# RMSNorm and matmul on one core: sixteen words of the output written at the outset, x in half-group loads throughout, finer last stores

## The chip, the cores and the metric

The kernel runs on one core of a Trainium2 chip. Its time is the device time of one execution in microseconds (us). Its compute engines are TensorE (PE), VectorE (DVE), ScalarE (ACT) and GpSimd (POOL); SyncE (SP) only waits and issues transfers. All transfers between the chip's main memory (HBM) and the on-chip buffer (SBUF) are carried by the core's 16 DMA engines.

## The reference

```python
batch, seq, dim, out_dim = 16, 1024, 512, 768

def reference(x, gamma, weight, eps):
    rms = np.sqrt(np.mean(x ** 2, axis=-1, keepdims=True) + eps)
    x_norm = x / rms * gamma
    return np.matmul(x_norm, weight).astype(np.float32)
```

x is 16384 rows (tokens) of 512 float32, 33.6 MB; the weight is 512 by 768 float32, 1.6 MB; the output is 16384 rows of 768 float32, 50.3 MB.

## The kernel before

**Tiling.** The rows form 128 tiles of 128 rows, and two tiles are a pair (`j`, tiles `2j` and `2j+1`). x is loaded in groups of 16 tiles (`XG`), the output is stored in groups of 8 (`OG`). Row numbering inside a group is `(p t)`: in x group 3, for instance, partition p holds 16 consecutive rows, one for each of the group's tiles. There are two x buffers (`xt`, 16 tiles each) and three output buffers (`ot`, 8 tiles each). `stretches` (L126) says in which pieces a group is transferred: x group 0 in loads of 2, 2, 4 and 8 tiles; groups 1, 2, 5, 6 and 7 in two loads of 8; groups 3 and 4, which the table leaves out, in one load of 16. Output group 0 goes in stores of 2, 2 and 4 tiles, group 1 and the last one (15) in two stores of 4, all others in one store of 8.

**Work on a tile.** POOL casts x to bf16. Three quarters of the tiles are turned by PE (transposes against the identity, L228) and copied out of PSUM by DVE (L237); the last four tiles of each group from the second on are turned by DVE alone (L269). ACT squares and sums each row (L194) and takes roots (L199), DVE takes the reciprocal (L201). PE multiplies by the weight, into which gamma has been folded at the start: four weight loads and eight matmuls a tile (L294, L298). `finish_tile` scales a result by the row's reciprocal root into `ot`: even tiles on ACT (L277), odd ones on DVE (L279). The last tile of each store also waits for the tile before it, so that one wait covers the store.

**Queues and order.** The order of work is written out by hand and recorded in `Order`: each operation names the cells that it reads and writes, and `emit` (L39) places a wait where an engine does not yet know that a needed operation has ended. `known` holds, for each engine, what it knows to be done: of engines a count, of transfers their own key. Transfers take a semaphore from a pool of slots. `last` (L81) collects the transfers that nobody awaits; `emit` returns their marks, and SP waits for those at the very end (L437). All loads and stores are issued by SP in program order, but for gamma's, which ACT issues first of all (L338), before it loads its activation table (L339). `load_until` issues the loads of x groups while tiles are worked on; `store(i)` (L286) issues a store when the last tile of its stretch is done. What SP waits for holds up everything behind it on SP.

Of the kernel before, what the change touches and what calls it, by code (L numbers as in the profile page):

```python
# [11 lines left out]
F32 = mybir.dt.float32  # L12
# [4 lines left out]
P = 128  # L17
# [3 lines left out]
class Order:  # L21
# [17 lines left out]
    def emit(self):  # L39
        nc = self.tc.nc  # L40
        streams = {id(e): n for n, e in enumerate((nc.tensor, nc.vector, nc.scalar, nc.gpsimd, nc.sync))}
        writer, readers = {}, {}
        known = [dict() for _ in streams]
        clocks, needs, place, slot_of, slots = [], [], [], {}, []
        count = [0] * len(streams)
        for n, (proc, engine, _, reads, writes) in enumerate(self.ops):
            at = streams[id(engine)]
            if proc is None:
                me, turn = ("transfer", n), 1
            else:  # L50
                count[at] += 1
                me, turn = at, count[at]
            written = {writer[cell] for cell in reads + writes if cell in writer}
            read = {d for cell in writes for d in readers.get(cell, ())}
            need = []
            for d in sorted(written | read, reverse=True):
                who, when = place[d]
                if who == me and (engine is nc.tensor or d not in written):
                    continue
                if known[at].get(who, 0) < when:  # L60
                    need.append(d)
                    for k, v in clocks[d].items():
                        known[at][k] = max(known[at].get(k, 0), v)
            if proc is None:
                free = [k for k, d in enumerate(slots) if known[at].get(("transfer", d), 0)]
                if free:
                    slots[free[0]] = n
                else:
                    slots.append(n)
                slot_of[n] = ("slot", slots.index(n))  # L70
            clock = dict(known[at])
            clock[me] = turn
            place.append((me, turn))
            clocks.append(clock)
            needs.append(need)
            for cell in reads:
                readers.setdefault(cell, []).append(n)
            for cell in writes:
                writer[cell], readers[cell] = n, []
        awaited = {d for need in needs for d in need}  # L80
        last = [n for n, (me, _) in enumerate(place) if not isinstance(me, int) and n not in awaited]  # L81
        sems, marks, done = {}, {}, {}
        for n in range(len(self.ops)):
            me = slot_of.get(n, place[n][0])
            if n in slot_of or n in awaited:
                if me not in sems:
                    sems[me] = self.tc.alloc_semaphore(f"done{len(sems)}")
                done[me] = done.get(me, 0) + (16 if n in slot_of else 1)
                marks[n] = (sems[me], done[me])
        for n, (proc, engine, issue, _, _) in enumerate(self.ops):  # L90
            for d in needs[n]:
                engine.wait_ge(*marks[d])
            ins = issue()
            if n in marks:
                ins.then_inc(marks[n][0], 16 if n in slot_of else 1)
        return [marks[n] for n in last]
# [3 lines left out]
def kernel(  # L100
# [8 lines left out]
    nc = tc.nc  # L109
    PE, DVE, ACT, POOL, SP = nc.tensor, nc.vector, nc.scalar, nc.gpsimd, nc.sync  # L110
    order = Order(tc)

    def run(engine, issue, reads=(), writes=()):
        order.add(1, engine, issue, reads, writes)

    x = x.flatten_outer_dims()
    out = out.flatten_outer_dims()
    N, D = x.shape
    _, O = out.shape
    K = D // P  # L120
    NT = N // P
    NP = NT // 2
    XG, OG = 16, 8
    AHEAD = 20

    def stretches(group, parts):  # L126
        first, size, i = {}, {}, 0
        for g in range(NT // group):
            for n in parts.get(g, [group]):
                for t in range(i, i + n):  # L130
                    first[t], size[t] = i, n
                i += n
        return first, size

    last = NT // OG - 1
    x_first, x_size = stretches(XG, {0: [2, 2, 4, 8], **{g: [8, 8] for g in (1, 2, 5, 6, 7)}})
    o_first, o_size = stretches(OG, {0: [2, 2, 4], 1: [4, 4], last: [4, 4]})

    def rows(ap, i, n):
        base, t = (x_first[i], x_size[i]) if i < XG else (i - i % XG, XG)  # L140
        return ap[base * P:(base + t) * P, :].rearrange("(p t) d -> p t d", t=t)[:, i - base:i - base + n, :]

    def sb(name, shape, dtype):
        return nc.alloc_sbuf_tensor(name, shape, dtype).ap()
# [14 lines left out]
    ot = [sb(f"ot{n}", [P, OG, O], F32) for n in range(3)]  # L159
# [7 lines left out]
    def cells(name, slot, i, n=1):  # L167
        return [(name, slot, t) for t in range(i, i + n)]
# [117 lines left out]
    def store(i):  # L286
        first, n = o_first[i], o_size[i]
        s = first // OG % 3
        if i == first + n - 1:
            src = ot[s][:, first % OG:first % OG + n, :]  # L290
            order.transfer(SP, lambda: SP.dma_start(out=rows(out, first, n), in_=src), reads=cells("ot", s, first % OG, n))

    def hold(lhsT, cell):
        run(PE, lambda: PE.ldweights(lhsT), [cell])  # L294
# [20 lines left out]
    def finish_tile(i, a, engine):  # L315
        s = i // OG % 3

        before = [("ot", s, i % OG - 1)] if i == o_first[i] + o_size[i] - 1 else []
        scale(engine, ot[s][:, i % OG, :], ops[a][:, :O], rstd[:, i:i + 1],
              [("ops", a, 0), ("ops", a, 1), ("rstd", i)] + before, [("ot", s, i % OG)])  # L320
        store(i)
# [14 lines left out]


    order.transfer(ACT, lambda: ACT.dma_start(out=g_row, in_=gamma.rearrange("(h w c) -> h w c", w=P, c=2)), writes=["g_row"])  # L338
    run(ACT, lambda: ACT.preload_act_table(AF.Sqrt))  # L339
    wv = weight.rearrange("(h w c) o -> w h (c o)", w=P, c=2)  # L340

# [131 lines left out]
```

## Time and profile before

| | us |
|---|---|
| median of 4 runs | 209.61 (209.52 to 210.35) |
| the profiled execution's own time | 209.52 |
| its span, first to last instruction | 207.6 |
| last compute instruction ends (DVE, L279) | 199.36 |
| last store issued by SP | 199.38 |
| last store landed (6.8 after its issue) | 206.2 |

| engine | busy us | share of the span |
|---|---|---|
| PE (matmul) | 194.5 | 94% |
| DVE | 149.4 | 72% |
| ACT | 144.6 | 70% |
| POOL | 59.9 | 29% |
| DMA, SP's queue | | 97.4% of 16 engines |

The mean granted TensorE clock is 0.984. The transfers move 85.62 MB at a mean of 412 GB/s. Busy time says how much of the span an engine worked, not that it set the end: where two resources are both nearly always busy, one must look at which of them works last, and at whether it ever stood idle before. A transfer has three moments: its issue on SP, its first packets on the DMA engines, and its landing, when its completion is counted on a semaphore.

### The profile page before, as it was taken

The numbers are of one execution on the slowest core, as the hardware profiler recorded it, in microseconds if no ns is written. First come the engines' busy times: TensorE is split into PE (matmuls) and PEld (weight loads), VectorE is DVE, ScalarE is ACT, GpSimd is POOL, SyncE is SP. The second block draws the span as 40 slices with busy tenths as digits, with TensorE's granted clock in tenths as the row PEclk, the third lists the DMA queues.
The fourth block names the chain that finished last, engine by engine and source line by source line (L and its number), as shares of the span: only waits on it lengthen the run. The fifth ranks groups of instructions, "written<-read, shape, count | busy, mean of one in ns | idle before, by whom it ended". The sixth has DMA issues, their size and how long they took to land.

```text
span 207.6 us, 2784 instructions
## 1 busy us (share of the span) xinstructions
PE 194.5 (94%) x1236; PEld 72.6 (35%) x717; DVE 149.4 (72%) x255; ACT 144.6 (70%) x343; POOL 59.9 (29%) x34
## 2 busy tenths in 40 slices
PE   7789999999999999999999999999999999999920
PEld 1223434433343333343334333443343334433300
DVE  0446466999579975999569975999569974999410
ACT  3598898777787687776877687677877788663310
POOL 2055742046200291005800670006600273000000
PEclk9999999999999999999999999999999999999985
DMA  6999999999999899999999999999999999997995
GB/s 221 398 445 436 369 410 436 428 429 422 438 458 442 368 439 429 448 395 447 425 420 429 428 440 425 412 437 429 439 409 433 425 453 410 445 421 298 450 381 230
DMA packets 5488, 85.62 MB, mean 412 GB/s; under 512 B 610, under 2 KB 612, under 8 KB 1380
## 3 DMA queue, kind: packets, MB, share of 16 engines
q1 hardware_dynamic: 5472, 85.46, 97.4%
q8 instruction: 7, 0.11, 0.2%
q14 instruction: 5, 0.04, 0.0%
q10 hardware_dynamic: 4, 0.00, 0.0%
HBM read 35.13 MB, written 50.33 MB: 412 GB/s over the span
## 4 chain that ended last, share of the span: by engine, by line
PE 89%; DMA 4%; SPq 1%; POOL 1%; DVE 0%; issue 0%
PE ps L298 78%; PE ps L228 10%; DMA xt<-in_x_dram 4%; SPq L343 1%; POOL xb L186 1%; DVE ot L279 0%; SPq L175 0%; SPq L468 0%; SPq L432 0%
## 5 line engine op out<-in xcount | busy, mean ns | idle before, releaser
L298 PE MATMUL ps<-w_bf,xT 128*128 128x512 bf16 (+1 forms) x800 | 147.6, 326 | 1.5 <-DVE w_bf L279 1.4
L277 ACT ACTIVATE ot<-ps,rstd 128x768 f32<-128x768 f32 x64 | 57.5, 899 | 43.6 <-PE ps L298 41.9
L194 ACT ACTIVATE jk<-xt 128x512 bf16<-128x512 f32 x128 | 78.8, 619 | 5.5 <-DMA xt<-in_x_dram 5.5
L186 POOL CAST xb<-xt 128x2048 bf16<-128x2048 f32 (+3 forms) x21 | 46.3, 2218 | 112.3 <-DMA xt<-in_x_dram 77.0
L279 DVE TENSOR_SCALAR ot<-ps,rstd 128x768 f32<-128x768 f32 x64 | 64.8, 1013 | 8.5 <-PE ps L298 7.8
L294 PEld LDWEIGHTS <-xT 128*128 128x128 bf16 x400 | 39.3, 98 | 60.0 <-issue 52.1
L228 PE MATMUL ps<-ident_f,xb 128*128 128x128 f32 x200 | 54.5, 277 | 0.9 <-POOL xb L186 0.9
L237 DVE COPY xT<-ps 128x1024 bf16<-128x1024 bf16 (+1 forms) x53 | 34.5, 654 | 25.1 <-PE ps L228 23.4
L269 DVE STREAM_TRANSPOSE xTq<-xq 32x256 f32<-32x256 f32 x112 | 48.8, 435 | 3.4
L228 PEld LDWEIGHTS ps<-ident_f,xb 128*128 128x128 f32 x200 | 28.2, 143 | 46.7 <-issue 43.2
L298 PE MATMUL ps<-w_bf,xTq 128*128 128x512 bf16 x224 | 42.8, 326 | 0.0
L194 ACT ACTIVATION_READ_ACCUMULATOR jk<-xt 128x1 f32 x128 | 24.3, 190 | 0.0
L294 PEld LDWEIGHTS <-xTq 128*128 128x128 bf16 x112 | 11.0, 98 | 14.5 <-issue 14.5
L258 POOL CAST xq<-xt 128x2048 bf16<-128x2048 f32 x7 | 13.3, 1893 | 0.0
L201 DVE RECIPROCAL rstd<-rms 128x8 f32<-128x8 f32 (+3 forms) x20 | 3.9, 192 | 7.4 <-ACT rms L199 7.2
L199 ACT ACTIVATE rms<-ssq,eps_sb 128x8 f32<-128x8 f32 (+3 forms) x20 | 6.0, 300 | 0.6
L298 PE MATMUL ps<-warm 128*128 128x512 bf16 x10 | 4.5, 590 | 1.4 <-DVE eps_sb L352 1.4
L277 ACT ACTIVATE w_bf<-w_f,g_sb 128x768 bf16<-128x768 f32 x2 | 1.9, 936 | 2.0 <-DMA w_f<-in_weight_dram 2.0
L375 DVE COPY g_sb<-ps 128x4 f32<-128x4 f32 x1 | 0.2, 163 | 3.1 <-PE ps L369 3.1
L279 DVE TENSOR_SCALAR w_bf<-w_f,g_sb 128x512 bf16<-128x512 f32 (+2 forms) x3 | 1.4, 482 | 1.5 <-DMA w_f<-in_weight_dram 1.5
L339 ACT ACT_TABLE_LOAD x1 | 1.3, 1283 | 1.5 <-SPq L432 1.5
L369 PEld LDWEIGHTS ps<-ident_f,g_row 2*128 2x128 f32 x2 | 0.3, 200 | 2.6 <-issue 2.6
(10 smaller groups left out, 2.0 us busy)
## 6 DMA issues: line engine op xcount, KB each, us to landing
out_dram<-ot SPq DMA_DIRECT2D x13, 3072.0 KB, 15.5
xt<-in_x_dram SPq DMA_DIRECT2D x11, 2048.0 KB, 20.0
xt<-in_x_dram SPq DMA_DIRECT2D x2, 4096.0 KB, 22.1
out_dram<-ot SPq DMA_DIRECT2D x5, 1536.0 KB, 10.1
w_f<-in_weight_dram SPq DMA_DIRECT2D x2, 768.0 KB, 6.1
out_dram<-ot SPq DMA_DIRECT2D x2, 768.0 KB, 14.8
xt<-in_x_dram SPq DMA_DIRECT2D x2, 512.0 KB, 5.4
xt<-in_x_dram SPq DMA_DIRECT2D x1, 1024.0 KB, 9.3
```

Source lines behind the costliest of these rows:

```text
L186: run(POOL, lambda: POOL.tensor_copy(out=xb[s][:, i % 8:i % 8 + n, :], in_=src), of, cells("xb", s, i % 8, n))
L194: run(ACT, lambda: ACT.activation(out=jk[j], in_=src[:, 0, :], func=AF.Square, accum_out=ssq[:, i:i + 1]), of, [("jk", j), ("ssq", i)])
L199: run(ACT, lambda: ACT.activation(out=rms[:, s], in_=ssq[:, s], func=AF.Sqrt, scale=1.0 / D, bias=eps_sb), [("ssq", t) for t in range(i, i ...
L201: run(DVE, lambda: DVE.reciprocal(out=rstd[:, s], in_=rms[:, s]), [("rms", i)], [("rstd", t) for t in range(i, i + n)])
L228: run(PE, lambda: PE.transpose(out=tp[b][:, t, h, :], in_=words[:, lo:lo + P], identity=ident_f), cells("xb", s, j % 4 * 2 + t) + ["ident" ...
L237: run(DVE, lambda: DVE.tensor_copy(out=dst[:, t:t + n, :], in_=src[:, t:t + n, :]), [("tp", b)], cells("xT", j % 4, t, n))
L258: run(POOL, lambda: POOL.tensor_copy(out=xq[s], in_=src), of, [("xq", s)])
L269: run(DVE, lambda: DVE.transpose(out=dst, in_=src), [("xq", s)], [("xTq", s)])
L277: run(ACT, lambda: ACT.mul(out=dst, in_=src, mul=r), reads, writes)
L279: run(DVE, lambda: DVE.tensor_single_scalar(out=dst, in_=src, scalar=r, op=mybir.AluOpType.mult), reads, writes)
L294: run(PE, lambda: PE.ldweights(lhsT), [cell])
L298: run(PE, lambda: PE.add_instruction(mybir.InstMatmult(name=nc.get_next_instruction_name(), engine=mybir.EngineType.PE, ins=[PE.lower_ap(r ...
```

## The change

The output's rows 0, 8, ..., 120 get a zero in their first column right after gamma's load, from ACT's queue; the first store (tiles 0 and 1, rows 0 to 255), which writes the same places, names the cell `marks` as written too, so that it waits for the sixteen words. x groups 3 and 4 are loaded in two halves like the others. Output group 14 goes in two stores of 4 tiles, group 15 in 4, 2 and 2. In `emit`, `last` is computed from the transfers that no engine's clock holds, instead of from those that nobody needs.

```diff
@@ emit
         awaited = {d for need in needs for d in need}
-        last = [n for n, (me, _) in enumerate(place) if not isinstance(me, int) and n not in awaited]
+        seen = {who for clock in known for who in clock}
+        last = [n for n, (me, _) in enumerate(place) if me not in seen and not isinstance(me, int)]
@@ tile_rmsnorm_matmul_kernel
-    x_first, x_size = stretches(XG, {0: [2, 2, 4, 8], **{g: [8, 8] for g in (1, 2, 5, 6, 7)}})
-    o_first, o_size = stretches(OG, {0: [2, 2, 4], 1: [4, 4], last: [4, 4]})
+    x_first, x_size = stretches(XG, {0: [2, 2, 4, 8], **{g: [8, 8] for g in range(1, NT // XG)}})
+    o_first, o_size = stretches(OG, {0: [2, 2, 4], 1: [4, 4], last - 1: [4, 4], last: [4, 2, 2]})
@@ store
-            order.transfer(SP, lambda: SP.dma_start(out=rows(out, first, n), in_=src), reads=cells("ot", s, first % OG, n))
+            order.transfer(SP, lambda: SP.dma_start(out=rows(out, first, n), in_=src), reads=cells("ot", s, first % OG, n),
+                           writes=["marks"] if first == 0 else [])
@@ after gamma's load
     order.transfer(ACT, lambda: ACT.dma_start(out=g_row, in_=gamma.rearrange("(h w c) -> h w c", w=P, c=2)), writes=["g_row"])
+
+    zeros = nc.const_aps.tensor(0.0, (16, 1), F32)
+    order.transfer(ACT, lambda: ACT.dma_start(out=out[:P, :1].rearrange("(e r) c -> e r c", r=8)[:, 0, :], in_=zeros, allow_slow_non_contiguous=True), writes=["marks"])
     run(ACT, lambda: ACT.preload_act_table(AF.Sqrt))
```

## The prediction

> **What bounds the kernel now.** The page comes first: PE is 94% busy, but the transfers on SP's queue fill 97.4% of 16 engines' time. The chain of waits cannot separate the two, since it starts from the last compute instruction, which ends at 199.36 us of a span of 207.6. So I read the end: SP's waits, then the windows.
>
> ```profile
> SPq L468 <- DMA out_dram<-ot: 5.9, 1, 5.9
> ```
>
> SP waits 5.9 us at its end for a store: what ends last is a transfer.
>
> ```profile
> 176.00:187.00 11.00, 11.00 (x75) 4.38 (x44) 10.43 (x20) 7.53 (x19) 0.00 (x0) 1.00 1.01 431
> 187.00:188.00 1.00, 1.00 (x9) 0.35 (x4) 0.93 (x3) 0.32 (x1) 0.00 (x0) 1.00 0.75 320
> 188.00:189.00 1.00, 1.00 (x8) 0.32 (x4) 0.97 (x2) 0.00 (x0) 0.00 (x0) 1.00 0.46 197
> 189.00:190.00 1.00, 1.00 (x8) 0.32 (x4) 0.97 (x2) 0.76 (x1) 0.00 (x0) 1.00 0.29 123
> 190.00:191.00 1.00, 1.00 (x9) 0.29 (x3) 0.93 (x3) 0.14 (x1) 0.00 (x0) 1.00 0.92 393
> 191.00:198.00 7.00, 7.00 (x45) 2.06 (x21) 3.51 (x5) 2.70 (x3) 0.00 (x0) 1.00 0.99 420
> 198.00:205.00 7.00, 0.30 (x2) 0.00 (x0) 1.02 (x1) 0.00 (x0) 0.00 (x0) 0.71 1.00 421
> 205.00:206.20 1.20, 0.00 (x0) 0.00 (x0) 0.00 (x0) 0.00 (x0) 0.00 (x0) 0.50 0.03 10
> ```
>
> Columns: the stretch, its length, busy time of PE, weight loads, DVE, ACT and POOL, clock, DMA share, GB/s. DMA is full at about 430 GB/s until 187, then its share falls in steps (0.75, 0.46, 0.29) and is back when the store of group 14, issued at 189.63 by SP's timeline, reaches the engines. Steps, not one drop: the engines run out of work at different times. Every transfer has 128 data packets and ends on each engine with one four-byte packet; in the packets' records those of the store before lie at 187.30 on the first engine and at 190.84 on the last. Most engines idle between, (1 − share) summed over 187 to 191 being 0.25+0.54+0.71+0.08 = 1.6 us; the last one never does, and its final four-byte packet is at 205.68 (the other fifteen: 205.22 to 205.35). Landing follows at 206.17 and the program's closing 1.4 us later. The bound is therefore **the slowest DMA engine, busy without a break to the end**; PE, fed throughout, is 6 us less late.
>
> Where does that engine lose time? Loads of 8 tiles need 4.87 us an engine (8 x 0.61). In the first load just before the first store the records show 5.58 us on the fastest engine (21.00 to 26.58) and 5.89 on the last (22.15 to 28.04): 0.71 and **1.02 us** too long. It shows in the windows, with nothing but that load in the queue:
>
> ```profile
> 20.00:24.00 4.00, 4.00 (x29) 1.86 (x18) 2.16 (x5) 3.90 (x12) 2.77 (x2) 1.00 0.98 418
> 24.00:25.00 1.00, 1.00 (x9) 0.41 (x5) 0.82 (x2) 0.36 (x1) 1.00 (x1) 1.00 1.22 377
> 25.00:26.00 1.00, 1.00 (x9) 0.40 (x4) 0.17 (x1) 1.00 (x3) 1.00 (x1) 1.00 0.81 213
> 26.00:27.00 1.00, 1.00 (x9) 0.37 (x4) 1.00 (x2) 1.00 (x5) 0.34 (x1) 1.00 0.88 346
> 42.00:50.00 8.00, 8.00 (x53) 2.91 (x29) 7.64 (x14) 5.80 (x13) 3.91 (x2) 1.00 1.00 422
> ```
>
> The rate halves at 25 us. On every engine the long packets are the two or three before the first output packet, whenever that engine gets there (24.06 at the earliest, 25.20 at the latest). At the next passage from load to store (in 42 to 50) the fast engines take 4.87 again, only the laggards are stretched by some 0.4. So the first approach to the output costs more than later ones. That it is the first write, and not the first read of `ot`, I infer.
>
> **The change, part by part.** *The sixteen words.* If a write that early takes over whatever the first store pays, the slowest engine gains up to 1.02 us, a fast one 0.71. No row shows a four-byte write to HBM from ACT's queue, so its cost in front of the loads is bounded: from 0.01 (a four-byte completion packet takes 0.009) to 1.0 us (gamma's first packet on that queue held its engine 0.999 us, and that engine began x 0.8 later than the others). I take 0.1: one tiny packet an engine, and gamma's second packet, which took 0.044, is nearest to it. On ACT the issue is one more like gamma's:
>
> ```profile
> 0.91 0.54 ACTq L338 DMA_DIRECT2D g_row<-in_gamma_dram  x1
> 1.49 1.28 ACT L339 ACT_TABLE_LOAD   x1 [1.49 <-SPq L432]
> 4.46 0.63 ACT L194 ACTIVATE jk<-xt 128x512 bf16<-128x512 f32 x1 [1.69 <-DMA xt<-in_x_dram]
> ```
>
> 0.54 us shifts the table load to 2.03–3.31; ACT then idles 1.69 us until x lands, so 1.15 of cover stay; without it the first squares, and with them root and first tile, would be late by 0.54. SP's weight issues run at the same time; if they were held up, 0 to 0.54 us of supply would be missing, which PE could not pass on to the end (6 us of slack), the slowest engine only if it ran dry.
>
> *The first store's wait.* Queued behind it on SP are all later stores and loads. It issues at 13.89; the words, issued by 2.1, need at most what 512 KB of x need (3.5 us from issue to landing), so they are there by 5.6: nothing, with 8 us to spare.
>
> *Groups 3 and 4 in halves.* Two more issues of about 1.0 us (a pair takes 1.93 to 2.17, the single ones 1.34 and 1.01) on SP, which then waits over 10 us for DVE: hidden. On an engine, sixteen packets of 32 KB (median 1.213) become 32 of 16 KB (0.611): 16 x 0.009 = 0.14 us at the medians, 0.09 at the means (1.242 against 2 x 0.624). PE never waits for those groups; earlier halves give nothing.
>
> *Finer stores.* 14's first half can go after tile 115 (DVE ends at 183.30), its second at 189.6, 15's at 194.2, 196.8 and 199.4. Packets: 24 KB 0.912 against 2 x 0.460, 12 KB 0.460 against 2 x 0.234: 8 x 0.008 twice, 0.13 us. Four more completions in all, 0.04. DVE's scalings of tiles 115 and 125, now the last of their stores, also wait for ACT's tile before; ACT was done at 181.24 and 195.34 (180.34 and 194.44 plus 0.90), DVE begins at 182.28 and 195.74: nothing. The idle 1.6 us is filled for the fast engines. The slowest gains nothing from that directly, but they stop setting 205.3 as a floor, and a gain of the slowest can then show whole. The new floor is the last 2-tile store: 199.38 + 0.9 (issue to first packets, as for group 14) + 8 x 0.234 + 0.5 = 202.7, far off.
>
> *The end's waits.* A transfer enters an engine's clock only through somebody's need for it or through a clock merged from there, so "in a clock" and "needed" are the same set: the new `last` picks the same kind of transfers. With finer stores they are six (13, twice 14, three times 15) instead of four. SP passed the three that were left after the last landing at 0.065 us each; two more are 0.13. More waits, not fewer.
>
> Against the finer pieces speaks the Trainium skill, "DMA: Bandwidth & Descriptors", section "Anatomy of one DMA": a fixed part of about 2.0 us for every DMA, fitted on GpSimd's path, and its "Rules for kernel authors" want 1 MiB or more in one; the last two stores have 0.75 MiB. Were that part paid serially by the four extra pieces, 8 us would be added and the kernel were far slower. Here transfers follow each other in a filled queue, 12 KB packets at the same rate as 24 KB ones, so I leave it out of the sum.
>
> *Sum* on the slowest engine: −1.02 + 0.10 + 0.14 + 0.13 + 0.04 + 0.13 = −0.5. To that I add an estimate: that engine lost another 2 us (0.4, 0.6, 0.6, 0.4) at later passages because it lagged; 0.31 less lag after the first (1.02 − 0.71) should take about as much off these, −0.3. Together **−0.8**: 209.52 − 0.8 = **208.7** (span 206.8). The profiled run lies 0.09 below the median, which I ignore.
>
> **The rivals.**
> 1. *The tail gives its gap in full.* Were the engines' load evened out, the 1.6 us of idleness would come off whole: 209.5 − 1.6 + 0.4 (finer pieces, waits) = 208.3, with half of the first-store gain, 0.5, 207.8. For it: the share drops at 187 to 190. Against it: one engine's records show no break.
> 2. *It does not do what it says.* The stall belongs to the first passage from load to store, or it only moves from 24 us to 2.5, equally on the DMA's path: nothing is gained, the finer pieces and waits stay, 209.52 + 0.44 = 210.0. For it: laggards are stretched at later passages, too, where no first write is left.
> 3. *Slower: the words block the start and the stall stays.* Sixteen packets on another queue go ahead of x and weights, and each holds its engine like gamma's, up to 1.0 us, with the slowest among them: 209.52 + 0.44 + 0.6 to 1.0 = 210.6 to 211.0. It decides (slower than a measurement's bound) once the words cost over 0.28 us an engine and nothing comes back at 24 us. For it: the 0.999; against it: gamma's second packet, 0.044.
>
> **How the numbers follow.** Forecast 0.45 (its own range 208.0 to 209.2), rival 1 0.15, rival 2 0.22, rival 3 0.18. A measurement tells about 0.3% (0.63 us) from no change: faster is below 208.98, slower above 210.24. Of the forecast 0.38 lies below, 0.07 within; rival 1 all below; rival 2 0.18 within, 0.04 above; rival 3 0.15 above, 0.03 within. That makes 0.53, 0.28, 0.19. The range reaches from rival 1 with most of the first-store gain (208.3 − 0.8 = 207.5) to just short of rival 3 (210.5).
>
> **What would show it.** In the profile after: the rate between 24 and 27 us at 420 or more instead of 213 to 377, and no new dip of that size at 2 to 4 us (rivals 2 and 3); the DMA share at 187 to 190 near 1; the last landing at about 205.3; six waits at the end, 0.3 us after it. Wrong would be: the dip still there, x's first landing (3.5 us after issue) later by over 0.5, or a share that still falls in steps before the last store while the end moves by more than 1 us.

## The result, and the profile after

The changed kernel takes **210.25 us** (median of 46 runs, 209.94 to 210.87); the kernel before takes 209.89 in the same sessions (209.41 to 210.62, 73 runs). The ratio is **1.0016**, 95% interval 1.0011 to 1.0021: 0.36 us more. The forecast was 208.7; it went as rival 2, which had 210.0. The profiled execution has a span of 208.4 us (before: 207.6).

First the place where the dip was to vanish, in the windows of the changed kernel. Columns as in the prediction: stretch, length, busy time of PE, weight loads, DVE, ACT and POOL, clock, DMA share, GB/s.

```profile
20.00:24.00 4.00, 4.00 (x29) 1.73 (x18) 2.30 (x4) 3.29 (x11) 2.76 (x2) 1.00 1.10 442
24.00:25.00 1.00, 1.00 (x9) 0.44 (x5) 0.09 (x2) 1.00 (x2) 1.00 (x1) 1.00 0.88 229
25.00:26.00 1.00, 1.00 (x9) 0.40 (x4) 0.90 (x2) 1.00 (x5) 0.60 (x1) 1.00 0.92 197
26.00:27.00 1.00, 1.00 (x9) 0.34 (x4) 0.72 (x1) 1.00 (x4) 0.00 (x0) 1.00 0.74 262
42.00:50.00 8.00, 8.00 (x53) 2.85 (x29) 7.57 (x16) 6.25 (x15) 3.60 (x1) 1.00 1.02 430
```

The dip is there, and in this profile deeper: 229, 197 and 262 GB/s where the kernel before had 377, 213 and 346. The words were written: the page's line on ACT's queue has 36 packets instead of 4.

```profile
q10 hardware_dynamic: 36, 0.00, 0.0%
```

That is 32 more: by their number, a word and a completion for each of 16 engines (the records do not name the engine). This agrees with the Trainium skill ("DMA: Bandwidth & Descriptors", section "Why a DMA increments its semaphore by 16 and not by 1"), by which the largest number up to 16 that divides the slowest dimension on both sides, here 16 itself, is the number of engines.

Now the tail, in the same windows.

```profile
187.00:188.00 1.00, 1.00 (x9) 0.29 (x3) 0.94 (x3) 0.00 (x0) 0.00 (x0) 1.00 0.98 418
188.00:189.00 1.00, 1.00 (x9) 0.29 (x3) 0.97 (x2) 0.50 (x1) 0.00 (x0) 1.00 0.92 393
189.00:190.00 1.00, 1.00 (x9) 0.29 (x3) 0.93 (x3) 0.41 (x1) 0.00 (x0) 1.00 0.98 418
190.00:191.00 1.00, 1.00 (x8) 0.29 (x3) 0.97 (x2) 0.00 (x0) 0.00 (x0) 1.00 0.95 406
191.00:198.00 7.00, 6.57 (x41) 1.86 (x19) 3.20 (x5) 2.70 (x3) 0.00 (x0) 1.00 1.01 432
198.00:205.00 7.00, 0.00 (x0) 0.00 (x0) 0.62 (x1) 0.00 (x0) 0.00 (x0) 0.80 0.75 317
205.00:206.20 1.20, 0.00 (x0) 0.00 (x0) 0.00 (x0) 0.00 (x0) 0.00 (x0) 0.50 0.16 67
```

From 187 to 191 the engines are full (0.46 and 0.29 became 0.92 and 0.98). The idleness has moved to 198 to 205 (0.75 instead of 1.00) and a rest of work is left after 205 (0.16 instead of 0.03): most engines are done early, a few are not, and the end waits for these. In the packets' records the four-byte packets that close the last store lie between 202.56 and 206.40 us, where in the kernel before fifteen of the sixteen lay within 0.13 us. SP's waits tell the same:

```profile
SPq L442 <- DMA out_dram<-ot: 7.4, 1, 7.4
SPq L93 <- DMA out_dram<-const-float32-0.0: 1.2, 1, 1.2
```

The last instruction of DVE ends 0.7 us earlier than before, and SP waits 1.5 us longer for the last landing (7.4 against 5.9). The wait for the words is over at 6.0 us, while SP's first store is issued at 13.15. On ACT the issue of the words is seen between gamma's and the table load:

```profile
1.50 0.34 ACTq L343 DMA_DIRECT2D out_dram<-const-float32-0.0  x1
1.87 1.28 ACT L344 ACT_TABLE_LOAD   x1 [1.87 <-issue]
4.17 0.63 ACT L195 ACTIVATE jk<-xt 128x512 bf16<-128x512 f32 x1 [1.02 <-DMA xt<-in_x_dram]
```

It took 0.34 us (0.54 foreseen), and 1.02 us of ACT's idle time before the first square are left.

### The profile page after: what moved, and what is told of

It is laid out like the page before. It is cut to its first block, busy times and chain, and to the rows that moved or that the text cites. A ratio compares the mean times of both kernels' runs of the same rounds, so it can differ in the third digit from the quotient of the medians.

```text
span 208.4 us, 2797 instructions
## 1 busy us (share of the span) xinstructions
PE 193.8 (93%) x1236; PEld 72.3 (35%) x717; DVE 149.4 (72%) x255; ACT 144.6 (69%) x343; POOL 60.0 (29%) x34
## 4 chain that ended last, share of the span: by engine, by line
PE 88%; DMA 4%; SPq 1%; POOL 1%; DVE 0%; issue 0%
PE ps L300 78%; PE ps L229 10%; DMA xt<-in_x_dram 4%; POOL xb L187 1%; DVE ot L280 0%; SPq L348 0%; SPq L176 0%; SPq L473 0%; SPq L437 0%
## 5 line engine op out<-in xcount | busy, mean ns | idle before, releaser
L300 PE MATMUL ps<-warm 128*128 128x512 bf16 x10 | 3.9, 531 | 1.4 <-DVE eps_sb L357 1.4
```

The costliest lines, as they stand in the source:

```text
L300: run(PE, lambda: PE.add_instruction(mybir.InstMatmult(name=nc.get_next_instruction_name(), engine=mybir.EngineType.PE, ins=[PE.lower_ap(r ...
```

## The experiments

Ratios are to the kernel before, run beside each on the same chip. One measure recurs, the **excess** of the load of tiles 24 to 31, the last before the first store: by how much more than 4.86 us the median over the engines of its closing four-byte packets follows that of the load before. It is read from the packets' records. 4.86 us is what other loads of 8 tiles take. A "closing" packet is the four-byte packet with which a transfer ends on an engine.

**Each part alone.** Four kernels: the sixteen words with the first store's wait, the finer stores, the halves of groups 3 and 4, and the changed kernel without the words.

```diff
 marks_only:      before + the words and the wait
 tail_only:       before + o_first, o_size = stretches(OG, {..., last - 1: [4, 4], last: [4, 2, 2]})
 halves_only:     before + {g: [8, 8] for g in range(1, NT // XG)}
 after_no_marks:  tail_only + halves_only
```

> The kernel before with the sixteen words and the first store's wait alone. Theory A (the words take over what the first store pays; the finer tail hides the gain in no way): the dip at 24 to 27 us is gone, the slowest engine is 1.0 us earlier, but the others still wait for group 14's store, so the end moves by -0.3 to -0.4 us only (ratio about 0.998). Theory B (the words cure nothing and cost nothing): dip as before, ratio 1.000 within 0.001. Theory C (the words hold the engines at the outset): first x load lands over 0.5 us later, ratio 1.002 to 1.005.

> The kernel before with group 14 stored in 4 and 4 tiles and group 15 in 4, 2 and 2, nothing else. Theory A (the slowest DMA engine sets the end and has no idle time to recover): DMA share near 1 from 187 to 191, falling in steps after 201 instead, last landing as before or up to 0.3 us later, ratio 1.000 to 1.002. Rival (the 1.6 us of idle engine time at 187 to 191 comes off): last landing 1.0 to 1.6 us earlier, ratio 0.993 to 0.996.

> The kernel before with x groups 3 and 4 in two loads each, nothing else. Theory A (32 KB and 16 KB packets cost the same, two more issues on SP are hidden): ratio 1.000 to 1.0005, +0.0 to 0.1 us. Rival (each extra transfer pays a fixed part serially on the engines): +0.5 us or more for each of the two, ratio above 1.004.

> The changed kernel without the sixteen words and without the first store's wait (halves and finer stores stay; the way in which the last waits are picked is the old one, which yields the same waits). If the words do nothing: ratio 1.001 to 1.002 like the changed kernel. If the words cost what the changed kernel lost: ratio 1.000 or below. If the words gain what the rest loses: 1.003 or more.

| kernel | median us | ratio, 95% interval | excess us, profiled run |
|---|---|---|---|
| before | 210.02 | | 0.85 |
| words alone | 209.97 | 0.9998 (0.9986 to 1.0010) | 0.97 |
| finer stores alone | 209.87 | 0.9995 (0.9985 to 1.0005) | 1.20 |
| halves alone | 210.10 | 1.0002 (0.9991 to 1.0014) | 1.03 |
| changed without words | 210.27 | 1.0014 (1.0003 to 1.0025) | 1.02 |
| changed (runs of the result, ratio to their own 209.89) | 210.25 | 1.0016 (1.0011 to 1.0021) | 1.30 |

The excess belongs to the single profiled run of each, that of before from the run shown in the prediction. The words do nothing that can be measured, neither good (theory A) nor bad (theory C). The stronger of the two comparisons is the changed kernel with and without them, 1.0016 against 1.0014: there the slowest engine sets the end, so a gain of it would show. The words alone, in a kernel with the coarse last stores, could not have moved the end by more than 0.3 to 0.4 us, as the expectation says. The halves and the finer stores by themselves do not change the time either, within 0.15%.

The halves are not without effect, though. In the profiles of words alone and of finer stores alone, which load group 4 in one piece, PE stands still once near 98 us, 1.6 and 1.1 us long: ACT has waited 3.9 and 3.4 us for that load, whose last engine is late. With the halves PE has no such wait (halves alone, changed without words, changed). The line of words alone:

```profile
PE ps L299 <- ACT ot L277: 1.6, 1, 1.6
```

In that profile the store of group 14 is issued at 190.52 instead of 189.63, all engines have run dry by then, and their last closing packets lie within 0.17 us (206.09 to 206.26): here the work on the tiles sets the end, and not the slowest DMA engine. In the kernel before the two limits are only 0.33 us apart (205.68 against 205.35).

With only the finer stores changed, the tail of the windows is that of the changed kernel:

```profile
187.00:191.00 4.00, 4.00 (x27) 1.28 (x14) 3.80 (x7) 1.68 (x2) 0.00 (x0) 1.00 1.01 430
191.00:201.00 10.00, 7.76 (x48) 2.25 (x23) 4.95 (x6) 2.70 (x3) 0.00 (x0) 1.00 0.97 409
201.00:203.00 2.00, 0.00 (x0) 0.00 (x0) 0.00 (x0) 0.00 (x0) 0.00 (x0) 1.00 0.98 409
203.00:205.00 2.00, 0.00 (x0) 0.00 (x0) 0.00 (x0) 0.00 (x0) 0.00 (x0) 0.64 0.34 141
205.00:206.20 1.20, 0.00 (x0) 0.00 (x0) 0.00 (x0) 0.00 (x0) 0.00 (x0) 0.50 0.05 20
```

Full at 187 to 191, then falling by steps after 203, and landed at 206.3 against 206.2. So the 1.6 us of idleness cannot be had by earlier stores alone: rival 1 falls.

**Is it the slowest engine?** The changed kernel without the store of group 8, 3 MB, so 7.3 us of each engine's work; those rows of the output stay unwritten.

```diff
-        if i == first + n - 1:
+        if i == first + n - 1 and first // OG != 8:
```

> The changed kernel without the store of output group 8 (3 MB of the output stay unwritten; all arithmetic is done). If the slowest DMA engine, busy without a break, sets the end: 7.3 us of its work go, the end falls to the floor of the last 2-tile store, some 3.5 to 4.3 us earlier (ratio 0.979 to 0.984). If the tail after the last compute instruction is latency that does not depend on the backlog: no change (0.998 to 1.000).

205.78 us, ratio 0.9803 (0.9787 to 0.9819): 4.1 us less than before and some 4.5 less than the changed kernel. The windows of its tail:

```profile
187.00:191.00 4.00, 4.00 (x26) 1.22 (x13) 3.84 (x6) 0.97 (x2) 0.00 (x0) 1.00 0.68 286
191.00:198.00 7.00, 6.34 (x39) 1.81 (x19) 3.21 (x5) 2.64 (x3) 0.00 (x0) 1.00 0.88 366
198.00:202.00 4.00, 0.00 (x0) 0.00 (x0) 0.45 (x1) 0.00 (x0) 0.00 (x0) 0.81 0.91 370
202.00:203.70 1.70, 0.00 (x0) 0.00 (x0) 0.00 (x0) 0.00 (x0) 0.00 (x0) 0.50 0.00 0
```

Here all engines run dry before the last stores come (0.68 and 0.88), so they start the last one together: its sixteen closing packets lie within 0.17 us (201.63 to 201.80) and it lands 3.7 us after its issue, against 8.2 us in the changed kernel. PE's work is unchanged. The bound of the prediction holds for the changed kernel: what an engine still has to carry sets the end, until the floor of the last small store is reached (202.7 foreseen, 202.2 measured).

**What does the dip hang on?** First, whether it comes at a moment counted from the launch. DVE clears an output buffer before SP may begin.

```diff
+    run(DVE, lambda: DVE.memset(ot[2], 0.0), [], cells("ot", 2, 0, OG))
...
-order.transfer(SP, lambda: SP.dma_start(out=dst, in_=rows(x, i, x_size[i])), writes=to)
+order.transfer(SP, lambda: SP.dma_start(out=dst, in_=rows(x, i, x_size[i])), reads=cells("ot", 2, 0) if i == 0 else [], writes=to)
```

> The kernel before, its transfers on SP held back by one large VectorE fill of an output buffer (some microseconds; the first x load's issue shows how many). If the dip hangs on the kernel's progress (position in the stream of transfers, work of an engine on a given tile), it moves later by the same delay. If it comes at a moment counted from the launch, it stays at 24 to 27 us, then in the midst of other transfers. The time grows by the delay.

216.75 us in a single execution, 6.9 more. SP's timeline and the windows:

```profile
7.79 0.38 SPq L175 DMA_DIRECT2D xt<-in_x_dram  x1
...
24.00:28.00 4.00, 4.00 (x28) 1.64 (x17) 2.51 (x4) 3.97 (x11) 3.38 (x2) 1.00 1.06 451
31.00:34.00 3.00, 3.00 (x21) 1.19 (x12) 1.61 (x2) 3.00 (x10) 1.21 (x1) 1.00 0.87 236
```

The first load is issued 6.85 us later (7.79 against 0.94), and the dip comes at 31 to 34 instead of 24 to 27. It hangs on the kernel's progress.

Then the first stores were made early, by way of ACT's queue, so that they run between the loads.

```diff
-            order.transfer(SP, lambda: SP.dma_start(...), reads=cells("ot", s, first % OG, n))
+            q = ACT if first < 4 else SP
+            order.transfer(q, lambda: q.dma_start(...), reads=cells("ot", s, first % OG, n))
```

> The kernel before, its first two stores issued from ACT's queue, so that they run between the loads from about 15 us on instead of behind them at 26.6. If the dip at 24 to 27 us belongs to the first write of the output or to the first passage from load to store, it comes at 14 to 19 us, and 24 to 27 runs at 420 GB/s or more. If it belongs to something else (a moment, another engine's work, the load itself), it stays at 24 to 27. Time: the same within 0.3% either way, faster by up to 0.4% if the dip goes altogether.

210.03 us, ratio 1.0002 (0.9985 to 1.0019). The windows:

```profile
14.00:16.00 2.00, 1.95 (x13) 0.84 (x9) 0.07 (x1) 1.73 (x6) 0.84 (x1) 1.00 1.02 401
16.00:18.00 2.00, 1.77 (x12) 0.61 (x7) 1.77 (x4) 0.69 (x1) 0.00 (x0) 1.00 1.01 366
24.00:28.00 4.00, 3.95 (x27) 1.71 (x17) 2.56 (x5) 3.83 (x12) 2.98 (x1) 1.00 1.02 431
56.00:60.00 4.00, 4.00 (x27) 1.53 (x15) 1.95 (x3) 3.09 (x9) 0.00 (x0) 1.00 1.07 375
66.00:70.00 4.00, 4.00 (x29) 1.65 (x17) 3.84 (x8) 3.10 (x9) 0.00 (x0) 1.00 0.88 270
```

The dip at 24 is gone, a shallower one lies at 14 to 18 where the early stores run: it belongs to the first stores, or to the first passage from loads to stores. But two others appear or deepen, at 56 to 60 (a passage from store to load) and at 66 to 70 (from load to store). The kernel before has there:

```profile
56.00:60.00 4.00, 4.00 (x28) 1.62 (x16) 2.58 (x5) 2.38 (x7) 0.00 (x0) 1.00 1.07 461
66.00:70.00 4.00, 4.00 (x28) 1.59 (x16) 3.80 (x9) 2.80 (x6) 0.00 (x0) 1.00 0.92 352
```

The time is the same, but it does not measure what the engines gained or lost: in this profile (210.78 us, the longest of its ten executions) x came later behind the stores, PE worked 16.2 of the 18 us from 12 to 30 (before: 17.6), group 14's store was issued at 190.93 (before: 189.63), and the last closing packets lie within 0.5 us.

Last, the words were made larger: a whole store of zeros over rows 0 to 255 as SP's first transfer (run twice), and whole rows 0 to 127 from ACT's queue.

```diff
 full_store_first, full_store_again:
+    run(DVE, lambda: DVE.memset(ot[2][:, :2, :], 0.0), [], cells("ot", 2, 0, 2))
+    order.transfer(SP, lambda: SP.dma_start(out=rows(out, 0, 2), in_=ot[2][:, :2, :]), reads=cells("ot", 2, 0, 2), writes=["marks"])
 rows_first:
+    run(DVE, lambda: DVE.memset(ot[2][:, :1, :], 0.0), [], cells("ot", 2, 0))
+    order.transfer(ACT, lambda: ACT.dma_start(out=out[:P, :], in_=ot[2][:, 0, :]), reads=cells("ot", 2, 0), writes=["marks"])
```

> The kernel before, with a whole store of zeros (768 KB, rows 0 to 255 of the output, from an output buffer that VectorE clears) as the very first transfer on SP, and the real first store waiting for it. If the dip before the first store is the price of a first write of ordinary size on every engine, for which words of four bytes were too small, it is gone from 24 to 32 us. If it belongs to the passage from load to store, it is there again, later by the delay at the start (2 to 4 us). Time: longer by about that delay.

> The kernel with the whole store of zeros at the very start, once more. If the smaller dip (median excess 0.36 us in the last load before the first store, against 0.8 to 1.3 without it) and the slow early packets (0.5 us for 6 KB against 0.234 later) are its doing, both come again; if it was chance, the excess is 0.8 or more.

> The kernel before, with the output's first 128 rows written whole as zeros (384 KB, 3 KB a packet, eight packets an engine) from ACT's queue at the outset, in place of the sixteen words, and the real first store waiting for it. If size is what the words lacked, the median engine's excess in the last load before the first store falls from 0.8 to 1.3 us (all profiles so far) to 0.5 or less, and the early rows take over 0.2 us a packet. If not, it stays at 0.8 or more. Time: not shorter in either case, since the early rows are paid in front.

| | us, one execution each | excess us |
|---|---|---|
| whole store first | 213.46 | 0.37 |
| the same once more | 213.54 | 0.27 |
| whole rows first | 210.87 | 0.08 |
| nine other profiles (all but those of loads from tile 8 on and of the first two stores on ACT's queue) | | 0.85 to 1.31 |

Windows of the first of them, at the early store and before the real one:

```profile
4.00:6.00 2.00, 2.00 (x7) 0.31 (x3) 0.00 (x0) 0.00 (x0) 0.00 (x0) 1.00 1.08 283
28.00:30.00 2.00, 2.00 (x15) 0.75 (x8) 1.14 (x2) 2.00 (x6) 1.36 (x1) 1.00 0.86 304
```

Of the early store's eight packets of 6 KB on each engine, nearly all of the first five take 0.23 to 0.26 us, little more than the usual 0.234, and the last three, just before the engine turns to x, about 0.5. And the windows of whole rows first, where x and the weights suffer before the rows come:

```profile
2.00:4.00 2.00, 1.79 (x5) 0.10 (x1) 0.16 (x2) 0.76 (x1) 0.00 (x0) 1.00 1.02 294
4.00:6.00 2.00, 2.00 (x7) 0.64 (x4) 0.16 (x1) 1.35 (x5) 1.17 (x2) 1.00 0.90 279
24.00:27.00 3.00, 2.95 (x22) 1.22 (x12) 1.83 (x4) 2.29 (x7) 3.00 (x1) 1.00 1.04 437
```

The first packet of a row is on its engine at 5.90 us, and all row packets take 0.121 us, not over 0.2 as expected. What is slow are packets of x and of the weights ahead of them. It is so at the dip, too: the long packets are loads ahead of the first output packet. So the long packets stand just ahead of a passage, whichever kind they are, and the first writes are not slow for being the first.

So writes of ordinary size at the outset do take the dip over, mostly or wholly; words of four bytes do not. And the price is paid on the spot. With whole rows first, the load of tiles 16 to 23 closes at 22.74 us (median engine) against 20.85 to 21.04 in the changed kernel and the four of the first table: 1.7 to 1.9 later, of which the 0.39 MB themselves are 0.9 at 430 GB/s. The other 0.8 to 1.0 is about what the dip had cost. Nothing of it comes back: when the store of group 13 closes, the median engine is at 190.08 us against 188.70 to 189.08 in the kernel before and those of the first table's parts, later by at least the rows' own bytes. The times in the table measure this less well. In all three runs the store of group 14 is issued late (191.41 to 194.01 us), all engines but at most the last have run dry by then, and their last closing packets lie within 0.3 us, so that the later work on the tiles sets the end.

**Loads and stores side by side.** In the first of these kernels all x loads from tile 8 on are issued from ACT's queue, in the second those of groups 2 to 7.

```diff
-        order.transfer(SP, lambda: SP.dma_start(out=dst, in_=rows(x, i, x_size[i])), writes=to)
+        q = ACT if i >= 8 else SP          # the second kernel: i >= 2 * XG
+        order.transfer(q, lambda: q.dma_start(out=dst, in_=rows(x, i, x_size[i])), writes=to)
```

> The kernel before, all x loads from tile 8 on issued from ACT's queue, so that on the engines loads and stores take turns instead of following each other in blocks. If the slowest engine's later losses (0.4 to 0.6 us at each passage from load to store, 2 us in all) belong to the passages, they go, and the end is 0.5 to 2 us earlier (0.990 to 0.998). If the engines' work is what it is, no change within 0.3%. If ACT's issues (0.5 to 1.0 us each) or stores that overtake loads starve PE: slower, by up to 1%.

> The kernel before, the loads of x groups 2 to 7 issued from ACT's queue; the start is as it was. From 30 us on the engines take turns between loads and stores. If what the slowest engine loses later belongs to whole blocks following each other, it is 0.5 to 2 us faster (0.990 to 0.998). If reads lose time wherever writes run beside them, the long packets spread over all engines and the time is the same or longer by up to 1% (1.000 to 1.010).

230.30 us, ratio 1.0978 (1.0949 to 1.1007), and 215.26 us, 1.0268 (1.0216 to 1.0321): both slower by more than any of the guesses. In the first, x loads take engine time from the weights at the start (landed at 10.5 and 17.3 us instead of 6.3 and 9.1). In the second, loads share the engines with stores and land a median of 26.3 us after their issue. The groups of its stretch from 70 to 90 us (idle time before, then what ended it):

```profile
L299 PE MATMUL ps<-w_bf,xT 128*128 128x512 bf16 (+1 forms) x59 | 10.9, 327 | 3.8 <-ACT ot L278 3.8
L195 ACT ACTIVATE jk<-xt 128x512 bf16<-128x512 f32 x12 | 7.4, 619 | 6.1 <-DMA xt<-in_x_dram 6.1
```

ACT waits 6.1 us for x, its scalings come late, and PE stands still for 3.8 us, which it did nowhere in that stretch of the kernel before. Here the single queue, with its loads ahead of the stores that come after them, keeps PE fed.

## Why the prediction failed

**The bound was right for the changed kernel.** The end waits for the slowest DMA engine; 7.3 us less work on the engines brings it forward by some 4.5 us, to the floor of the last store, and earlier stores for the others by nothing. With the coarse last stores the work on the tiles is a limit close behind, and in several of the experiments it sets the end.

**The step that failed is the first term of the sum**: "If a write that early takes over whatever the first store pays, the slowest engine gains up to 1.02 us". In place of −1.02 the runs show 0: words alone 0.9998 (0.9986 to 1.0010), the changed kernel 1.0016 with them and 1.0014 without, the excess 0.97 and 1.30 us with them, 0.85 to 1.20 in the others of the first table. Two things were missed. Writes of four bytes do not take the price over; whole rows and whole stores do. And where they do, the price moves to the front of the same queues, on the path of the same engines: it is not saved. Rival 2 had said so ("it only moves"), and I gave it half the chance of the forecast. With this term goes the −0.3 that I had added for the lag at later passages.

**The cost terms came out about right as a sum.** What remains of it without the gain and without the words' 0.10 was 0.44 us; measured is 0.36 (0.23 to 0.44). That may be luck, for no run shows a single term: the finer stores (0.9995) and the halves (1.0002) alone show nothing, and together 1.0014 (1.0003 to 1.0025), within what their intervals allow. Which terms make up the 0.36 stays open. The Trainium skill gives a fixed part of about 2.0 us a DMA, fitted on GpSimd's path ("DMA: Bandwidth & Descriptors", section "Anatomy of one DMA"). The prediction had set it aside, and four transfers more cost nothing near 2.0 us apiece here.

**The rest.** The words' own cost: not measurable, at the low end of 0.01 to 1.0. ACT's issue and the first store's wait: hidden as said, the words landing at 6.0 instead of by 5.6. The halves: their cost is hidden, but "PE never waits for those groups; earlier halves give nothing" was read from the one profile of the kernel before, and it does not hold in those of words alone and finer stores alone, where PE waits 1.6 and 1.1 us. The finer stores: they fill the gap of the fast engines and nothing else. The last waits: six instead of four, with the new way of picking them (changed) as with the old (changed without words). SP's records show five of them passed in 0.31 us after the first, which had waited for the last landing, against three in 0.18; 0.13 had been foreseen.

**What stays open** is why the engines lose time at passages. The dip at the first store is tied to the first writes of ordinary size or to the first passage between loads and writes; no run separates the two. Later passages lose as much in some kernels: at 56 and 66 us with the early stores, and at 148 and 158 us with group 8's store left out. There 24 KB packets take up to 1.81 us at 149 instead of 0.912, and 16 KB ones 0.74 to 1.64 at 158 to 161 instead of 0.611. In the kernel before mainly the laggards lost at such passages (the load closing at 68 to 71: 0.2 us too long on the median engine, 1.0 on the last). In the two kernels with the dear later passages engines had run dry shortly before, at 51 and at 142 us, waiting for the next store: at the lowest 6 and 7 packets are in flight instead of 16. The kernel before has no such moment between 30 and 187 us. That is an observation, and no run tests whether it makes a passage dear.

## What to carry to other kernels

Where transfers fill all DMA engines, look at when the engines finish a transfer one by one: if the slowest has no idle time, finer stores or earlier issues for the others bring nothing, and only less work on the engines does. A price that is paid by every engine on the same path is not saved by paying it earlier; whether it is where the engines stand idle, no run here shows. Before an experiment's time is read as the price of what it changed, look at which limit sets its end: where all engines close the last store together, it is the work that came before its issue. A single ordered queue can be worth more than two, as here, since it decides which transfer comes first.

## What the runs showed of the hardware

The 16 engines drift apart: in the kernel before the closing packets of the first load lie within 0.6 us and those of a store at 187 us within 3.5, in the changed kernel those of a store at 173 us within 4.3. Instruction blocks of 16 KB travel on the same engines and hold one of them for 0.9 to 1.0 us each in the kernel before, seven times in a run: while such a block is in flight, the records show 15 data packets under way instead of 16. Packets just before the first passage between loads and writes are long, 0.5 us for 6 KB where 0.234 is usual. And the start is not the same in every profile: the second weight load's issue took 1.12 us on SP in the profile shown of before and 0.42 in most others. With the halves the last compute instruction then came 0.7 to 0.9 us earlier, with no gain at the end; with words alone and finer stores alone it came 0.9 and 0.5 us later, behind PE's wait near 98 us.
